# Memory's input and first weights take the places of x while the last projection pair runs

## The chip, the core and the metric

The kernel runs on one core of a Trainium2 chip. Five engines work side by side, each with its own queue of instructions in a fixed order: TensorE (PE; matmuls, with weight loads shown as PEld), VectorE (DVE), ScalarE (ACT), GpSimd (POOL) and SyncE (SP, which here issues all transfers). An instruction starts when those ahead of it in its queue have started and the tiles that it needs are ready; until then its queue stands. The metric is the device time of one execution in microseconds (us), lower is better.

## What is computed

One layer of a streaming encoder for 1024 prompt tokens and 64 sample tokens, width 1024, in fp32 accuracy. In outline:

```
h  = rms_norm(x);  p = h @ w_in                    # q, k, v of 8 A heads and 8 B heads, forget logits
x += concat(o_A, o_B) @ w_o                        # A: chunk band attention, B: forgetting attention
kv = rms_norm(mem) @ w_mkv                         # memory: 256 tokens, 4 heads of 256
mk, mv = rms_norm(kv[:, :1024] by head), kv[:, 1024:]
x += softmax(rms_norm(rms_norm(x) @ w_mq) @ mk.T / 16) @ mv @ w_mo
x += (silu(conv3(gate)) * value) @ w_down          # gate, value = rms_norm(x) @ w_up
```

The sample tokens do the same with keys and values from caches.

## The kernel before

**Exactness.** Each fp32 factor is split in a rounded part (hi, dtype F32R) and the rest (lo); a product is three matmuls, hi*hi, hi*lo and lo*hi. A split is one instruction on ACT (hi) and one on DVE or POOL (lo).

**The pairs.** The projection runs over eight pairs of heads p (0 to 3 of kind A, 4 to 7 of kind B) and, in each, over eight blocks t of 128 tokens. `products(p, t)` makes 24 matmuls of 384 columns (tile pj, line 299) from x's parts (xhi, xlo) and the pair's weights (whi, wlo). `proj` normalises q and k and turns them (tq, line 326). Woven between the matmuls of block t are the `substeps()` of the attention of blocks already projected, as an object `Attn(p, g, h)` for each group g of two blocks and head h: scores (tile S, line 499), their maximum (DVE, line 502), exponential (ACT, line 504), division (ACT or POOL), turning (PT, line 539; split by ACT, line 540, and DVE, line 541) and the product with v (tile O, one bank; line 554), which ACT (otmp, line 563) and DVE (mix, line 564) take out of the bank. `proj_sample` projects the sample tokens at a pair's end (line 347; sm, line 351).

**The drain.** After the last pair, attention has four substeps left. `step(n, subs)` weaves n pieces of the memory projection with one of them; `LEFT` holds the four n.

**Memory.** The projection of the 256 memory tokens has 16 units (n, t): eight blocks n of 256 columns of w_mkv, two blocks t of 128 tokens. A unit is four pieces of six matmuls of 256 columns (`mem_piece`, line 679), 384 in all. Its input is loaded in two halves (line 655), scaled and split into tiles mhi and mlo (`gained`, ACT line 265, DVE line 266). A block of weights is loaded in two halves (mwraw, line 661) and split in four pieces, mwhi on ACT (line 668) and mwlo on DVE and POOL in turn (line 669). `mem_end` normalises a unit into kv and stores it (out_mk, line 702); `mem_turn` turns it (PT, line 720) and stores it (kmd, line 723).

**Samples.** Eight samples follow, one for each pair. Each loads q, k, v of the sample (sqd, svn), its bias (s, from negs or rows), keys (kraw) and values (vraw) of the caches, splits them, and runs scores, exponential, turns, O and a last turn of the result su (line 857). They run as steps x; `PER[x]` says how many memory pieces are woven into step x. When no piece is left, the output product (line 948, tile a) starts.

**Order and memory.** A scheduler at build time fixes every queue's order from the program's order and the tiles that come free; a tile of a pool takes the place of one with the same tag that has been released. x's parts lie in two tiles [128, 8, 1024], which are released, with the pair weights, when all eight pairs are done (`left.close()`); memory's tiles are placed in that space afterwards.

Of the kernel before, what the change touches and what calls it, by code (L numbers as in the profile page):

```python
# [15 lines left out]
P = 128  # L16
# [10 lines left out]
LEFT = (0, 0, 0, 15)  # L27
PER = (4, 8, 9, 12, 6, 5, 6, 0, 0)
# [13 lines left out]
def hybrid_step(ctx: ExitStack, tc: tile.TileContext, i: dict, o: dict):  # L42
# [3 lines left out]
    def f32(ap):  # L46
        return ap.bitcast(F32)
# [125 lines left out]
    def split_col(c, k, raw):  # L173
        dst = [xs[:, k, a] for a in range(2)] if c == 4 else [a[:, k, c * 256:(c + 1) * 256] for a in x2]
        split_x(*dst, raw[:, k % 4], k, c == 0)
# [412 lines left out]
    def scale_gain():  # L588
# [5 lines left out]
             6: lambda: ([], norms(7, 8) + columns(4, 0) + columns(4, 1))}  # L594
    forgetting = []
    for p, np_ in zip(PAIRS, PAIRS[1:] + (None,)):
# [45 lines left out]
    left.close()  # L642


    left = ExitStack()
# [3 lines left out]
    mem = [mp.tile([P, KT, 256], F32R, name=f"m{n}") for n in ("hi", "lo")]  # L649
    gmk = mp.tile([P, 256], F32, name="gmk")  # L650
    nc.sync.dma_start(gmk, i["g_mk"].broadcast_to([P, 256]))

    def load_mem(z):
        raw = wk.tile([P, N], F32, name="s", bufs=4)[:, :1024].rearrange("p (k t) -> p k t", k=4)
        nc.sync.dma_start(raw, i["memT"][4 * z:4 * z + 4].rearrange("k p t -> p k t"))
        for k in range(4):
            gained((mem[0][:, 4 * z + k], mem[1][:, 4 * z + k], raw[:, k], gcol[:, 3, 4 * z + k:4 * z + k + 1], ALL))

    def load_wm(n, z):
        raw = mp.tile([P, 4, 256], F32, name="mwraw", bufs=2)  # L660
        nc.sync.dma_start(raw.rearrange("p k c -> p (k c)"), i["w_mkv"][n, z])
        wraw[n, z] = raw

    def split_wm(n, y):
        raw = wraw[n, y // 2][:, 2 * (y % 2):2 * (y % 2) + 2]
        hi = mp.tile([P, 2, 256], F32R, name="mwhi", bufs=6)
        lo = mp.tile([P, 2, 256], F32R, name="mwlo", bufs=6)
        act.copy(hi, raw)
        (dve if y % 2 else pool).tensor_tensor(lo, raw, f32(hi), op=ALU.subtract)
        wm.setdefault(n, []).append((hi, lo))  # L670

    wraw, wm, mpj = {}, {}, {}

    def mem_piece(n, t, c):
        if c == 0:
            mpj[n, t] = bank("pj")
        for m in range(6 * c, 6 * c + 6):
            k, (a, b) = m // 3, SPLIT[m % 3]
            mm = pe.matmul(mpj[n, t][:, :256], mem[a][:, k, t * P:(t + 1) * P], wm[n][k // 2][b][:, k % 2], start=m == 0, stop=m == 3 * KT - 1)
            if n + t + m == 0:  # L680
                tc.keep_in_program_order(mm)
# [203 lines left out]

    load_wm(0, 0)
    load_mem(0)
    load_wm(0, 1)
    load_mem(1)
    split_wm(0, 0)  # L890
    split_wm(0, 1)
# [1028 lines left out]
```

## Time and profile before

| | |
|---|---|
| time, median of 3 runs | 1780.92 us (1779.07 to 1783.11) |
| span of the profiled execution, first to last instruction | 1782.6 us |
| PE busy in the span | 1717.3 us, 12432 matmuls |
| DVE, ACT, POOL busy | 1217.0, 943.4, 646.1 us |
| moved by DMA | 199.88 MB, 112 GB/s in the mean |

The profile is of one execution. The time around its span is not shown apart: the span lies inside the range of the three runs, 1.7 us over their median, and the prediction's sum is made against it. In a row of a timeline stand: start, duration, engine, line, operation, out<-in, count, and in brackets the idle time ahead of it and what ended it. In a table of stretches each engine has its busy time and the number of its instructions, then the clock that PE was granted (1.00 is full), the DMA engines' busy share and GB/s. In a row of a tile's instructions the durations are ns, least/median/most.

### The profile page before, as it was taken

What the parts mean: (1) busy time and instruction counts of PE and PEld (TensorE: products, weight loads), DVE (VectorE), ACT (ScalarE), POOL (GpSimd) and SP (SyncE); (2) the same over time, 40 slices, a digit from 0 to 9 for tenths busy, and PEclk for the clock granted to TensorE, in tenths of its full rate; (3) what the DMA queues carried; (4) which work ended last, traced back from release to release, by engine and by line L of the source; (5) the groups of instructions that cost most, each with busy time, mean ns of one, the idle gap of its engine ahead of it and who ended that gap; (6) DMA issues with size and microseconds to landing.
All of it is one profiled execution on the core that took longest, in us unless ns stands there. A gap on an engine that the chain in (4) does not pass through costs nothing.

```text
span 1782.6 us, 34013 instructions
## 1 busy us (share of the span) xinstructions
PE 1717.3 (96%) x12432; PEld 1668.7 (94%) x12432; DVE 1217.0 (68%) x2659; ACT 943.4 (53%) x2074; POOL 646.1 (36%) x931
## 2 busy tenths in 40 slices
PE   7898999999998898999999999999999999999999
PEld 6888999999997787999999999999999999999999
DVE  5768667677677687533444379877777777649986
ACT  6756667677677577434555456433333333434432
POOL 3656667878777443443443611100000000000000
PEclk8999999999999899999999999999999999999999
DMA  7322122122112577641111563222222222693332
GB/s 246 99 63 62 59 77 79 49 74 77 50 55 81 175 259 248 194 140 46 54 54 54 153 217 103 76 80 73 83 82 89 82 73 73 226 339 130 118 105 88
DMA packets 136696, 199.88 MB, mean 112 GB/s; under 512 B 21240, under 2 KB 77688, under 8 KB 136528
## 3 DMA queue, kind: packets, MB, share of 16 engines
q1 hardware_dynamic: 136528, 197.70, 35.1%
q8 instruction: 98, 1.61, 0.4%
q14 instruction: 70, 0.57, 0.1%
HBM read 155.35 MB, written 45.44 MB: 113 GB/s over the span
## 4 chain that ended last, share of the span: by engine, by line
PE 49%; DVE 2%; issue 1%; POOL 1%; ACT 1%; DMA 0%; SPq 0%; DVEq 0%; POOLq 0%; ACTq 0%
PE W L1475 25%; PE W L1799 13%; PE pj L948 7%; PE S L1218 1%; PE tq L1254 1%; PE O L1254 1%; PE W L948 1%; POOL lo L930 1%; PE PT L1241 0%; DMA f<-x2d 0%; PE O L1218 0%; POOL s L1233 0%; PE PT L1199 0%; DVE lo L930 0%; ACT hi L929 0%
## 5 line engine op out<-in xcount | busy, mean ns | idle before, releaser
L299 PE MATMUL pj<-whi,xhi 128*128 128x384 f32 (+1 forms) x512 | 195.9, 383 | 2.2 <-ACT xhi L130 1.9
L299 PE MATMUL pj<-wlo,xhi 128*128 128x384 f32 (+1 forms) x512 | 176.9, 346 | 4.5 <-POOL wlo L123 4.5
L299 PE MATMUL pj<-whi,xlo 128*128 128x384 f32 (+1 forms) x512 | 176.3, 345 | 0.6 <-DVE xlo L131 0.6
L1581 POOL COPY s<-gp 128x2 f32<-128x2 f32 x22 | 15.8, 719 | 335.9 <-DVE gp L1580 335.9
L1475 PE MATMUL W<-h,hi 128*128 128x272 f32 x704 | 134.4, 288 | 1.4 <-ACT qlo L1611 1.4
L504 ACT ACTIVATE s<-s,mx 128x640 f32<-128x640 f32 (+7 forms) x128 | 94.4, 737 | 77.8 <-DVE mx L502 77.0
L1799 PE MATMUL W<-f,hi 128*128 128x272 f32 x672 | 127.1, 287 | 0.0
L541 DVE TENSOR_TENSOR ptl<-PT,pth 128x512 fp32r<-128x512 f32 (+2 forms) x192 | 99.4, 522 | 38.8 <-ACT pth L540 36.5
L1475 PEld LDWEIGHTS W<-h,hi 128*128 128x128 f32 x704 | 110.8, 188 | 1.7 <-ACT qlo L1611 1.6
L540 ACT CAST pth<-PT 128x512 fp32r<-128x512 f32 (+2 forms) x192 | 84.8, 449 | 43.8 <-PE PT L539 41.9
L299 PEld LDWEIGHTS pj<-wlo,xhi 128*128 128x128 f32 x512 | 99.6, 194 | 6.2 <-POOL wlo L123 6.1
L1799 PEld LDWEIGHTS W<-f,hi 128*128 128x128 f32 x672 | 105.3, 188 | 0.0
L299 PEld LDWEIGHTS pj<-whi,xhi 128*128 128x128 f32 x512 | 99.4, 194 | 4.4 <-ACT xhi L130 2.4
L1475 PE MATMUL W<-h,lo 128*128 128x272 f32 x352 | 101.8, 289 | 0.0
L299 PEld LDWEIGHTS pj<-whi,xlo 128*128 128x128 f32 x512 | 98.1, 192 | 1.8 <-DVE xlo L131 1.6
L539 PE MATMUL PT<-ident,s 128*128 128x128 f32 x528 | 90.5, 278 | 7.7 <-DVE ptl L541 7.3
L1799 PE MATMUL W<-f,lo 128*128 128x272 f32 x336 | 96.7, 288 | 0.0
L1339 ACT CAST hi<-raw 128x512 fp32r<-128x512 f32 x68 | 42.2, 621 | 98.5 <-PE W L1475 58.7
L948 PE MATMUL pj<-a,hi 128*128 128x384 f32 (+1 forms) x352 | 89.1, 336 | 2.5 <-ACT hi L929 1.6
L499 PE MATMUL S<-kh,q 128*128 128x256 f32 (+1 forms) x304 | 77.5, 280 | 13.1 <-DVE mx L502 13.1
L507 POOL TENSOR_SCALAR s<-s,ssum 128x640 f32<-128x640 f32 (+6 forms) x96 | 70.7, 738 | 47.5 <-DVE ssum L505 36.7
L554 PE MATMUL O<-pth,v 128*128 128x256 f32 (+1 forms) x304 | 78.0, 281 | 8.4 <-ACT mhi L265 7.7
(552 smaller groups left out, 6049.5 us busy)
## 6 DMA issues: line engine op xcount, KB each, us to landing
raw<-in_w_down_dram SPq DMA_DIRECT2D x45, 256.0 KB, 2.9
wraw<-in_w_dram SPq DMA_DIRECT2D x56, 192.0 KB, 2.5
raw<-in_w_up_dram SPq DMA_DIRECT2D x41, 256.0 KB, 2.7
h<-ad SPq DMA_DIRECT2D x32, 272.0 KB, 5.2
mwraw<-in_w_mkv_dram SPq DMA_DIRECT2D x16, 512.0 KB, 6.2
raw<-in_w_mo_dram SPq DMA_DIRECT2D x32, 256.0 KB, 3.2
kvraw<-in_w_down_dram SPq DMA_DIRECT2D x32, 256.0 KB, 3.1
ad<-t SPq DMA_DIRECT2D x22, 272.0 KB, 2.1
```

What stands on the lines that cost most here:

```text
L299: pe.matmul(pj[:, :nw], x2[a][:, k, t * P:(t + 1) * P], wt[k][b][:, :nw], start=n == 0, stop=n == 3 * KT - 1)
L499: pe.matmul(sp[:, a:a + (k1 - k0) * P], q, kk[:, h, src], start=m == 0, stop=m == 1)
L504: act.activation(s[:, :n], s[:, :n], ACT.Exp, bias=mx, scale=-1.0, accum_out=sm)
L507: pool.tensor_scalar(s[:, :n], s[:, :n], sm, 1.0, op0=ALU.mult, op1=ALU.mult)
L539: pe.transpose(pt[:, b - ch[0]], self.s[j][:, (b - w0) * P:(b - w0 + 1) * P], ident)
L540: act.copy(hi[:, f:f + n, j], pt[:, f:f + n])
L541: dve.tensor_tensor(lo[:, f:f + n, j], pt[:, f:f + n], f32(hi[:, f:f + n, j]), op=ALU.subtract)
L554: pe.matmul(op[:, cols], groups[p, b // 2].v[:, b % 2, h].rearrange("p a d -> p (a d)"), pt[:, x, cols], start=b == self.full[0] and m == ...
L948: pe.matmul(out()[:, :cn], w[a][:, k % 4], x[b][k][:, c0:c0 + cn], start=k == 0 and (a, b) == SPLIT[0], stop=k == KT - 1 and (a, b) == SPL ...
L1339: act.copy(hi, t)
L1475: pe.matmul(w[:, z, :Q], a(p, j), rights[j][b][:, z * Q:z * Q + Q], start=fresh and begin and j == 0 and x == 0, stop=final and end and j ...
L1799: pe.matmul(ws[m][:, z, :Q], la[p][:, m * P:(m + 1) * P], ra[b][:, z * Q:z * Q + Q], start=first and y == 0 and what in opening, stop=fina ...
```

## The change

x's parts become sixteen tiles of [128, 4, 256]: for each of hi and lo, four column blocks of 256 tokens times two halves of the depth, with the tags xhi and xlo, eight places each. When the last pair has used a tile for the last time, its place goes to one of memory's tiles of the same size: input (mraw), its parts, weights (mwraw), their parts. The pool of x stays open until the last memory piece; the pair weights' pool alone is closed. The input's loads and splits and the loads and splits of weight blocks 0 and 1 are called beside the last pair's blocks t = 2 to 7 (`beside`); the input no longer passes through a tile s of the attention. `LEFT` and `PER` spread the 65 memory steps anew: 23 in the drain instead of 15. A matmul that was held to the program's order no longer is.

```
-LEFT = (0, 0, 0, 15)
-PER = (4, 8, 9, 12, 6, 5, 6, 0, 0)
+LEFT = (4, 5, 6, 8)
+PER = (4, 6, 7, 8, 6, 5, 6, 0, 0)
...
-    wp = left.enter_context(tc.tile_pool(name="wp", bufs=1, side="left"))
-    x2 = [xp.tile([P, KT, T], F32R, name=f"x{n}") for n in ("hi", "lo")]
+    weights = ExitStack()
+    wp = weights.enter_context(tc.tile_pool(name="wp", bufs=1, side="left"))
+    def quarter_tile(part, name, dt=F32R):
+        return xp.tile([P, 4, 256], dt, name=name, tag=f"x{part}", bufs=8)
+    x2 = {}
+    def x_part(a, k, t0, n):
+        return x2[a, t0 // 256][k // 4][:, k % 4, t0 % 256:t0 % 256 + n]
...
-            pe.matmul(pj[:, :nw], x2[a][:, k, t * P:(t + 1) * P], wt[k][b][:, :nw], start=n == 0, stop=n == 3 * KT - 1)
+            pe.matmul(pj[:, :nw], x_part(a, k, t * P, P), wt[k][b][:, :nw], start=n == 0, stop=n == 3 * KT - 1)
...
+    def load_mem(z):
+        raw = raw_of["m", z] = quarter_tile(QUARTERS[z], "mraw", F32)
+        nc.sync.dma_start(raw, i["memT"][4 * z:4 * z + 4].rearrange("k p t -> p k t"))
+    def split_mem(k):
+        z, raw = k // 4, raw_of["m", k // 4]
+        if k % 4 == 0:
+            mem[z] = [quarter_tile(x, f"m{x}") for x in QUARTERS]
+        gained((mem[z][0][:, k % 4], mem[z][1][:, k % 4], raw[:, k % 4], gcol[:, 3, k:k + 1], ALL))
+    def load_wm(n, z):
+        raw = raw_of[n, z] = quarter_tile(QUARTERS[z], "mwraw", F32)
+        nc.sync.dma_start(raw.rearrange("p k c -> p (k c)"), i["w_mkv"][n, z])
...
+    beside = {2: [lambda z=z: load_mem(z) for z in range(2)], 4: [lambda z=z: load_wm(0, z) for z in range(2)],
+              6: [lambda z=z: load_wm(1, z) for z in range(2)], 7: [lambda y=y: split_wm(0, y) for y in range(4)]}
+    for z in range(2):
+        beside.setdefault(4 + z, []).extend(lambda k=k: split_mem(k) for k in range(4 * z, 4 * z + 4))
...
+            if np_ is None:
+                subs += beside.get(t, [])
...
-    left.close()
+    weights.close()
...
-            if n + t + m == 0:
-                tc.keep_in_program_order(mm)
...
-                if n == 0 and t == 0:
-                    if c < 2:
-                        split_wm(0, c + 2)
-                if n < 7:
-                    if t == 0 and c in (1, 2):
-                        load_wm(n + 1, c - 1)
-                    if t == 1:
-                        split_wm(n + 1, c)
+                if n < 7 and t == 1:
+                    split_wm(n + 1, c)
+                if n in range(1, 6) and t == 0 and c in (1, 2):
+                    load_wm(n + 2, c - 1)
...
-    load_wm(0, 0)
-    load_mem(0)
-    load_wm(0, 1)
-    load_mem(1)
-    split_wm(0, 0)
-    split_wm(0, 1)
+    for z in range(2):
+        load_wm(2, z)
```

The changed kernel's line numbers differ: the attention's are 11 higher (499 becomes 510, 554 becomes 565), those of kv, the samples and kmd 18 higher (702 becomes 720), and memory's functions now stand earlier (655, 661, 668, 669 and 679 become 611, 621, 629, 630 and 637).

The first place is ACT's queue at the end of the last pair, behind the sample's projection (sm). Before:

```order
L351 COPY sm<-pj 64x384
L265 ACTIVATE q<-tq,gd 128x2x128
L265 ACTIVATE mhi<-s,gcol 128x256
L233 ACTIVATE sq<-sm 64x256
L355 ACTIVATE vf<-sm,rstd_81 64x128
L265 ACTIVATE mhi<-s,gcol 128x256 x3
L668 CAST mwhi<-mwraw 128x512 x2
L563 COPY otmp<-O 64x256
L540 CAST pth<-PT 128x4x128 x2
```

In the changed kernel, at the same place:

```order
L362 COPY sm<-pj 64x384
L276 ACTIVATE q<-tq,gd 128x2x128
L244 ACTIVATE sq<-sm 64x256
L366 ACTIVATE vf<-sm,rstd_81 64x128
L574 COPY otmp<-O 64x256
L515 ACTIVATE s,ssum<-s,mx 128x896
L551 CAST pth<-PT 128x4x128
L520 ACTIVATE s<-s,ssum 128x896
L551 CAST pth<-PT 128x4x128
```

The splits of memory's input and of weight block 0 have moved ahead, between the blocks of the last pair; eight mhi and eight mwhi now stand before sm on ACT, eight mlo and four mwlo on DVE, four mwlo on POOL.

The second place is PE's queue in the drain, ahead of the first group of eight turns. Before:

```order
L554 MATMUL O<-pth,v 128x256
L554 MATMUL O<-ptl,v 128x256
L554 MATMUL O<-pth,v 128x128
L554 MATMUL O<-ptl,v 128x128
L539 MATMUL PT<-ident,s 128x128 x8
L554 MATMUL O<-pth,v 128x256
L499 MATMUL S<-kh,q 128x256
```

In the changed kernel, behind the same four O:

```order
L565 MATMUL O<-pth,v 128x256
L565 MATMUL O<-ptl,v 128x256
L565 MATMUL O<-pth,v 128x128
L565 MATMUL O<-ptl,v 128x128
L637 MATMUL pj<-mwhi,mhi 128x256
L637 MATMUL pj<-mwlo,mhi 128x256
L637 MATMUL pj<-mwhi,mlo 128x256
```

Groups of memory matmuls now stand between attention's groups. Counted over the whole order, 96 memory matmuls stand ahead of the last O (6 before), 128 from there to the first sample's turn of su (165 before), and 160 behind that (213 before).

The third place is SP's queue where the first sample's transfers stand. Before:

```order
L737 DMA sqd<-sqk 64x512
L702 DMA out_mk_dram<-kv 128x256
L661 DMA mwraw<-in_w_mkv_dram 128x1024
L723 DMA kmd<-kt 128x2x128
L739 DMA svn<-sv 64x128
L702 DMA out_mk_dram<-kv 128x256
L750 DMA kraw<-in_cbk_dram 128x1024
L723 DMA kmd<-kt 128x2x128
L750 DMA kraw<-in_cbk_dram 128x1024
L702 DMA out_mk_dram<-kv 128x256
L723 DMA kmd<-kt 128x2x128
L754 DMA vraw<-in_cbv_dram 128x512 x2
```

In the changed kernel:

```order
L720 DMA out_mk_dram<-kv 128x256
L741 DMA kmd<-kt 128x2x128
L755 DMA sqd<-sqk 64x512
L757 DMA svn<-sv 64x128
L768 DMA kraw<-in_cbk_dram 128x1024 x2
L772 DMA vraw<-in_cbv_dram 128x512 x2
```

Keys and values of the first sample stand together, behind the third pair of stores of kv and ahead of the fourth. Twelve of the sixteen weight loads (mwraw) now stand ahead of them, where six did.

More of the change, by code (lines that the diff above doesn't have):

```diff
@@ L173, in split_col @@
     def split_col(c, k, raw):
-        dst = [xs[:, k, a] for a in range(2)] if c == 4 else [a[:, k, c * 256:(c + 1) * 256] for a in x2]
+        if c < 4 and k % 4 == 0:
+            for a, part in enumerate(("hi", "lo")):
+                x2.setdefault((a, c), []).append(quarter_tile(part, f"x{part}"))
+        dst = [xs[:, k, a] for a in range(2)] if c == 4 else [x_part(a, k, c * 256, 256) for a in range(2)]
         split_x(*dst, raw[:, k % 4], k, c == 0)
@@ L641, in hybrid_step @@
             forgetting = forget()
-    left.close()
-    left = ExitStack()
+    weights.close()
     mp = left.enter_context(tc.tile_pool(name="mp", bufs=1, side="left"))
@@ L648, in hybrid_step @@
     vmd = dram.tile([2, P, T], F32, name="vmd")
-    mem = [mp.tile([P, KT, 256], F32R, name=f"m{n}") for n in ("hi", "lo")]
     gmk = mp.tile([P, 256], F32, name="gmk")
     nc.sync.dma_start(gmk, i["g_mk"].broadcast_to([P, 256]))
[L653 to L679, printed above, removed]
-            if n + t + m == 0:
-                tc.keep_in_program_order(mm)
     kvs, stores = {}, []
```

16 lines of the change are left out of this document (added).

## The prediction

> **What bounds the kernel now.** First the page of the profile: span, busy shares, and the 40 slices of 44.6 us each.
>
> ```profile
> span 1782.6 us, 34013 instructions
> PE 1717.3 (96%) x12432; PEld 1668.7 (94%) x12432; DVE 1217.0 (68%) x2659; ACT 943.4 (53%) x2074; POOL 646.1 (36%) x931
> PE   7898999999998898999999999999999999999999
> PEclk8999999999999899999999999999999999999999
> ```
>
> TensorE (PE) is the bound. It is below 9 tenths only at the start and in slices 13 to 16 (535 to 713 us), where its clock also falls. The change moves work only there, so I cut that place into stages, by what PE's timeline shows: the last pair, the attention that drains after it (566.3 is the end of the last projection, 601.1 the last O), the stretch to the end of the first sample's attention, and the other samples up to the first output product. A second table shows the clock.
>
> ```profile
> core 0: us, PE busy (x) PEld busy (x) DVE busy (x) ACT busy (x) POOL busy (x), PEclk, DMA share, GB/s
> 510.00:566.30 56.30, 55.66 (x384) 53.59 (x383) 37.43 (x109) 37.40 (x94) 39.77 (x80) 1.00 0.12 36
> 566.30:601.10 34.80, 22.53 (x142) 20.25 (x141) 25.55 (x47) 23.45 (x48) 19.39 (x26) 0.80 0.60 172
> 601.10:640.10 39.00, 34.46 (x243) 31.24 (x243) 29.27 (x76) 24.04 (x66) 17.32 (x20) 0.96 0.67 225
> 640.10:705.10 65.00, 60.25 (x427) 52.36 (x425) 46.18 (x116) 47.38 (x122) 25.43 (x21) 1.00 0.77 241
> ```
>
> ```profile
> 570.00:580.00 10.00, 1.92 (x9) 1.42 (x8) 7.99 (x13) 8.26 (x19) 7.23 (x10) 0.77 0.70 223
> 580.00:590.00 10.00, 7.78 (x43) 6.62 (x42) 8.62 (x16) 6.52 (x14) 6.81 (x8) 0.72 0.20 64
> 590.00:600.00 10.00, 8.03 (x51) 7.41 (x52) 5.98 (x13) 5.64 (x10) 3.95 (x5) 0.83 0.82 216
> ```
>
> In the last pair PE is full (55.66 of 56.30) and the other three engines have 16 to 19 us free each, the DMA nearly all. In the drain PE idles 12.3 us of 34.8. The PE rows say where:
>
> ```profile
> 578.01 0.55 PE L554 MATMUL O<-pth,v 128*128 128x256 f32 x1 [7.72 <-ACT mhi L265]
> ...
> 579.52 0.42 PE L499 MATMUL S<-kh,q 128*128 128x256 f32 x1
> 579.74 0.41 PE L499 MATMUL S<-kl,q 128*128 128x256 f32 x1
> ...
> 590.14 0.55 PE L539 MATMUL PT<-ident,s 128*128 128x128 f32 x3 [1.35 <-DVE ptl L541]
> 591.94 0.66 PE L539 MATMUL PT<-ident,s 128*128 128x128 f32 x4 [1.14 <-DVE ptl L541]
> ...
> 599.61 0.28 PE L679 MATMUL pj<-mwlo,mhi 128*128 128x256 f32 x1
> 599.73 0.28 PE L679 MATMUL pj<-mwhi,mlo 128*128 128x256 f32 x1
> ```
>
> One gap of 7.72 us; then matmuls of 256 columns start every 0.22 us (579.52 to 579.74) instead of every 0.12 (599.61 to 599.73). The gap's cause stands in ACT's and DVE's rows:
>
> ```profile
> 569.71 0.51 ACT L265 ACTIVATE mhi<-s,gcol 128x256 fp32r<-128x256 f32 x1 [0.62 <-DMA s<-in_memT_dram]
> 573.05 1.14 ACT L668 CAST mwhi<-mwraw 128x512 fp32r<-128x512 f32 x2 [1.04 <-DMA mwraw<-in_w_mkv_dram]
> 574.22 0.37 ACT L563 COPY otmp<-O 64x256 f32<-64x256 f32 x1
> 574.22 3.19 DVE L669 TENSOR_TENSOR mwlo<-mwraw,mwhi 128x512 fp32r<-128x512 f32 x1 [1.70 <-ACT mwhi L668]
> 577.45 0.42 DVE L564 TENSOR_TENSOR mix<-O,otmp 64x256 f32<-64x256 f32 x1
> ```
>
> The one O bank is free only after otmp and mix. Both stand in their queues behind the preparation of memory's input (mhi) and weights (mwhi, mwlo), which waits for its loads; the DVE split then took 3.19 us. So PE waits for work that it needs only at 599.5.
>
> **The drain (566.3 to 601.1).** The change takes all of this preparation out of the two queues: the 7.7 us gap goes, and what is late next is the chain scores, maximum, exponential, turn that the pauses of 1.35 and 1.14 show. A mean clock of 0.80 over 34.8 us is 13.9 us at half speed, of which some 11 lie outside the gap; PE idles in part of them anyway, so I give them 3 us (0 to 5.6). That leaves 24.1 us. Into it come, by the order, 96 memory matmuls before the last O instead of 6: 90 at 0.12 are 10.8. Attention's own 136 at 0.12 are 16.3. PE work is 27.1, over 24.1, so the stretch becomes PE's, with 1.5 us of pauses left: 28.6, that is -6.2. If all the added matmuls fit into pauses it is 24.1 (-10.7); if none does, 34.9 (+0.1).
>
> That the clock is lost with the gap is also what the Trainium skill says ("TensorE: Matmul & The Clock Gate", Part 1): about 3.4 us with little work halve it, about 3.4 us of work restore it. By that rule a drain whose pauses stay short runs at 1.00, and the 3 us are safe. The trace agrees at the long gap; but 590 to 600 shows 0.83 after two pauses of little over 1 us, so by the row some of the 3 us may come back.
>
> **To the first sample's end (601.1 to 640.1).** The order has 128 memory matmuls here instead of 165: 37 at 0.12, -4.4, since PE is busy 34.46 of 39.00. The rest:
>
> ```profile
> PE PT L720 <- DVE kv L701: 4.3, 4, 1.6
> 607.19 0.34 SPq L702 DMA_DIRECT2D out_mk_dram<-kv  x1
> 609.00 1.24 SPq L723 DMA_DIRECT2D kmd<-kt  x1
> 611.52 0.43 SPq L750 DMA_DIRECT2D kraw<-in_cbk_dram  x1
> 617.57 0.37 SPq L723 DMA_DIRECT2D kmd<-kt  x1
> 617.99 0.97 SPq L754 DMA_DIRECT2D vraw<-in_cbv_dram  x2
> ```
>
> PE waits 4.3 us for kv, the normalised memory keys; three of six such turns now fall into the drain beside attention, I take 2 us off. SP issues in order: the first sample's keys and values leave at 611.5 and 618.0, behind stores that wait for kv. Now they stand ahead of the fourth such store, so they can leave about 4 us after the last O instead of 10.4 and 16.9. PE waits little for them today, having memory matmuls to do, so I take 1.7 us: -8.1 in all. Bounds: -4.4 (all waits stay) to -13 (kv waits and sample waits go).
>
> **The other samples (640.1 to 705.1).** 160 memory matmuls instead of 213: 53 at 0.12 are 6.4. PE is busy 60.25 of 65.00, so nearly all should show: -6.0. But each sample is a chain through ACT and DVE, and the matmuls cover it: if the chains set the pace, 0. The weight loads now run ahead (12 of 16 issued before the first sample's keys, 6 before), which relieves a DMA share of 0.77; no PE wait on it is in the rows, so I count only up to 2 us: -8.
>
> **The last pair (510 to 566.3).** It takes the moved work:
>
> ```profile
> L265 ACT ACTIVATE mhi<-s,gcol x8: 491/499/516, 569.7 to 577.8; 128x256 fp32r<-128x256 f32 x8
> L266 DVE SCALAR_TENSOR_TENSOR mlo<-s,gcol,mhi x8: 469/476/486, 570.2 to 580.6; 128x256 fp32r<-128x256 f32 x8
> L668 ACT CAST mwhi<-mwraw x32: 602/617/631, 573.1 to 686.4; 128x512 fp32r<-128x512 f32 x32
> L669 DVE TENSOR_TENSOR mwlo<-mwraw,mwhi x16: 677/789/3195, 574.2 to 687.1; 128x512 fp32r<-128x512 f32 x16
> L669 POOL TENSOR_TENSOR mwlo<-mwraw,mwhi x16: 1262/1292/1749, 575.6 to 686.1; 128x512 fp32r<-128x512 f32 x16
> ```
>
> By the order eight mhi and eight mwhi go to ACT (4.0 + 4.9 = 8.9 us), eight mlo and four mwlo to DVE (3.8 + 3.2 = 7.0), four mwlo to POOL (5.2). Each engine has at least 16 us idle there, which is the cover; the loads have the DMA at 0.12. But the three run in order, and a turn that comes late stops PE. SP carries eight loads past the pair's stores, some waiting for a split; vf and ko have two buffers each, so a late store would hold ACT and POOL. I take +2. No PE work leaves this pair, so a gain is excluded; the upper bound is ACT's 8.9 laid bare.
>
> Sixteen tiles for x instead of two: the same matmuls in the same order up to the last pair, every slice inside one tile; 0. memory's raw input no longer takes two of the four s buffers: counted with the pauses.
>
> **Sum.** -6.2 - 8.1 - 6.0 + 2.0 = -18.3 on the span of 1782.6: 1764.3. The runs have a median of 1780.9 (1779.1 to 1783.1), 1.7 under that span, so the median becomes 1762.6; I say 1762.5.
>
> **Rivals.** (1) The chains set the pace of the samples: the last -6.0 is 0 and the stretch before gives only -4.4. For it: PT and ptl pauses wherever memory matmuls are few. Against: 60.25 of 65.00 busy. -6.2 - 4.4 + 2 = -8.6: 1772. (2) The pauses vanish everywhere: -10.7 - 13 - 8 + 0 = -31.7: 1749. Against it: kv's turns still stand behind only 18 to 29 matmuls, 2 to 3.5 us, where PE waits up to 1.6 today. (3) DVE is held in the last pair:
>
> ```profile
> L669 DVE TENSOR_TENSOR mwlo<-mwraw,mwhi 128x512 fp32r<-128x512 f32 x3 | 6.3, 2096 | 1.7 <-ACT mwhi L668 1.7
> L669 DVE TENSOR_TENSOR mwlo<-mwraw,mwhi 128x512 fp32r<-128x512 f32 x13 | 11.1, 856 | 0.5 <-ACT mwhi L668 0.5
> ```
>
> The same DVE split averages 2.10 us in the drain and 0.86 after it (0.68 at best); the longest, 3.19, runs while POOL works. The last pair has POOL busy 39.77 of 56.30. If each of the twelve moved DVE instructions is held as the three were (1.4 over the best) and PE pays, the pair costs 17 us: net -3.3, 1777.6. If each is held as the worst was (2.5), 30 us: net +9.7, 1790.6, slower. It decides from 1.7 us each. Against it: after the drain the hold is 0.18 a piece beside a POOL at 0.4, and DVE has 19 us free. The Trainium skill has such a rule ("SBUF — State Buffer", Who interferes with whom): a DVE instruction with two inputs in SBUF and a POOL instruction exclude each other for the whole instruction; the 3.19 us row agrees, the mean of 0.86 says that it seldom bites. (4) The gap only moves: memory matmuls stand right behind the last turns of the pair in PE's queue, and if their parts are late PE stops there instead: no change, 1781. Against: the parts are issued two steps and more earlier.
>
> **How the numbers follow.** Forecast as summed 0.62; (1) 0.16; (2) 0.12; (3) 0.06, half of it slower; (4) 0.04. The range 1746 to 1776 reaches from (2), with a little below it, past (1); it leaves out (3), (4) and the upper bounds all at once (0.1 - 4.4 + 0 + 8.9 = +4.6). About 0.2%, 3.6 us, is what a measurement here tells from no change. Faster 0.90; same 0.05; slower 0.05.
>
> **What would show it.** Right: no PE gap over 2 us after the last pair, clock near 1.00 from 566 to 600; mhi and the first mwhi before 566; memory matmuls between S and PT; last O near 597, the first sample's su turned near 628, the first output product near 687; the sample's keys issued within 5 us of the last O. Wrong: the last projection later than 569, DVE mwlo of 2 us in the last pair, PE waits on su, kclo or kv that grow by as much as the matmuls leave.

## The result, and the profile after

The changed kernel takes 1784.2 us (median of 21 runs, 1780.6 to 1785.9); the kernel before, run beside it, takes 1780.06 (21 runs, 1777.7 to 1783.5). The ratio is 1.0019 [1.0013, 1.0026]: slower by 0.19%, a little under what the prediction took as measurable, where 1762.5 was forecast.

The page of the changed kernel: span, PE's busy share, its 40 slices, the granted clock.

```profile
span 1781.2 us, 34032 instructions
PE 1714.3 (96%) x12432; PEld 1666.1 (94%) x12432; DVE 1216.3 (68%) x2659; ACT 942.3 (53%) x2074; POOL 644.8 (36%) x931
PE   7898999999999888999999999999999999999998
PEclk8999999999999998999999999999999999999999
```

PE's row was below 9 in slices 13, 14 and 16; now it is in 14, 15 and 16 (44.5 us each) and in the last. The clock's dip has moved from slice 14 (579 to 624 us) to slice 16 (668 to 712), into the samples. The four stages of the changed kernel (last pair, drain, to the first su, other samples), by the columns of the prediction's tables:

```profile
496.10:570.40 74.30, 69.94 (x474) 65.53 (x473) 55.09 (x146) 55.82 (x135) 57.64 (x99) 1.00 0.36 109
570.40:602.80 32.40, 29.30 (x239) 27.84 (x238) 25.58 (x59) 22.91 (x56) 17.55 (x25) 1.00 0.41 115
602.80:635.90 33.10, 28.65 (x210) 25.65 (x209) 25.81 (x70) 20.73 (x55) 14.67 (x18) 0.99 0.81 258
635.90:704.50 68.60, 58.88 (x365) 50.22 (x363) 46.23 (x107) 44.75 (x113) 24.52 (x22) 0.90 0.64 201
```

Before, the same stages took 68.8, 34.9, 39.0 and 65.1 us. The drain's clock went from 0.80 to 1.00 and its 7.72 us gap is gone, as forecast. The last pair got 5.5 us longer, and the samples 3.5 us longer, with 53 memory matmuls fewer and a clock of 0.90 where there was 1.00.

The profile of before that the prediction used was of a long execution: its span and the 1.8 us around it make 1784.4, 4.3 over the median of 21 runs. The first experiment below (e3) has the order of before in every queue; its stages, also of one execution, show how far two such profiles differ:

```profile
496.90:565.60 68.70, 67.94 (x473) 65.48 (x472) 48.38 (x134) 48.44 (x119) 50.68 (x96) 1.00 0.15 46
565.60:598.30 32.70, 20.79 (x143) 17.86 (x142) 22.28 (x49) 23.48 (x48) 18.64 (x24) 0.84 0.64 184
598.30:635.70 37.40, 33.45 (x244) 29.92 (x243) 29.44 (x75) 24.02 (x65) 18.33 (x23) 1.00 0.71 236
635.70:700.90 65.20, 60.64 (x429) 52.50 (x426) 46.37 (x117) 47.48 (x122) 25.46 (x21) 1.00 0.74 240
```

The drain of before was 2.2 us longer and the next stretch 1.6, with the same order: chance between executions. Against e3 the change moves the stages by +5.6, -0.3, -4.3 and +3.4: +4.4 in all, which fits the 4.1 us between the medians.

### The profile page after: what moved, and what is told of

Its sections match the earlier page's. It is cut to its first block, busy times and chain, and to the rows that moved or that the text cites. A ratio compares the mean times of both kernels' runs of the same rounds, so it can differ in the third digit from the quotient of the medians.

```text
span 1781.2 us, 34032 instructions
## 1 busy us (share of the span) xinstructions
PE 1714.3 (96%) x12432; PEld 1666.1 (94%) x12432; DVE 1216.3 (68%) x2659; ACT 942.3 (53%) x2074; POOL 644.8 (36%) x931
## 4 chain that ended last, share of the span: by engine, by line
PE 51%; DVE 1%; POOL 1%; issue 1%; ACT 0%; DVEq 0%; POOLq 0%; ACTq 0%
PE W L1485 25%; PE W L1809 13%; PE pj L958 7%; PE W L958 2%; PE S L1228 1%; PE tq L1264 1%; PE O L1264 1%; POOL lo L940 1%; PE PT L1251 0%; PE O L1228 0%; PE PT L1209 0%; POOL s L1243 0%; DVE f L1350 0%; ACT hi L939 0%; DVE qhi L1337 0%
## 5 line engine op out<-in xcount | busy, mean ns | idle before, releaser
L550 PEld LDWEIGHTS PT<-ident,s 128*128 128x128 f32 x528 | 65.5, 140 | 14.9 <-DVE ptl L552 9.1
```

The costliest lines, as they stand in the source:

```text
L550: pe.transpose(pt[:, b - ch[0]], self.s[j][:, (b - w0) * P:(b - w0 + 1) * P], ident)
```

## The experiments

All runs in one table: us by stage, the clock and the memory matmuls (M) in the samples and M in the drain, each from the one profile of that kernel. Ratios are against the kernel before, run beside each.

| kernel | median us, runs | ratio, 95% interval | pair | drain | to su | samples | clock | M drain, samples |
|---|---|---|---|---|---|---|---|---|
| before | 1780.06, 21 | | 68.8 | 34.9 | 39.0 | 65.1 | 1.00 | 6, 213 |
| changed | 1784.20, 21 | 1.0019 [1.0013, 1.0026] | 74.3 | 32.4 | 33.1 | 68.6 | 0.90 | 96, 160 |
| e3 | 1780.19, 11 | 1.0000 [0.9991, 1.0008] | 68.7 | 32.7 | 37.4 | 65.2 | 1.00 | 6, 213 |
| e1 | 1771.91, 5 | 0.9950 [0.9937, 0.9962] | 75.5 | 26.1 | 34.7 | 62.2 | 1.00 | 45, 208 |
| e2 | 1786.08, 7 | 1.0029 [1.0017, 1.0040] | 68.8 | 41.2 | 32.8 | 68.5 | 0.95 | 96, 165 |
| e4 | 1782.82, 11 | 1.0014 [1.0006, 1.0023] | 68.9 | 41.1 | 34.4 | 64.6 | 0.95 | 96, 161 |
| e6 | 1778.54, 11 | 0.9989 [0.9980, 0.9997] | 71.9 | 32.8 | 34.9 | 66.8 | 0.93 | 54, 204 |
| e7 | 1778.80, 12 | 0.9997 [0.9988, 1.0005] | 68.9 | 33.6 | 31.9 | 71.4 | 0.97 | 62, 214 |
| e8 | 1782.89, 12 | 1.0014 [1.0004, 1.0025] | 76.8 | 31.9 | 34.0 | 67.0 | 0.95 | 54, 204 |
| e9 | 1775.91, 11 | 0.9979 [0.9971, 0.9988] | 78.1 | 26.1 | 34.8 | 62.4 | 1.00 | 45, 208 |
| e12 | 1787.63, 5 | 1.0043 [1.0031, 1.0055] | 73.8 | 33.6 | 37.0 | 68.8 | 0.95 | 96, 171 |
| e11 | 1775.85, 7 | 0.9975 [0.9963, 0.9987] | 73.6 | 29.5 | 33.9 | 65.8 | 0.97 | 48, 216 |
| e13 | 1773.15, 6 | 0.9962 [0.9949, 0.9975] | 72.4 | 28.4 | 33.7 | 64.6 | 1.00 | 48, 216 |
| e14 | 1771.02, 5 | 0.9950 [0.9938, 0.9963] | 73.1 | 26.0 | 35.0 | 62.2 | 1.00 | 45, 208 |
| e15 | 1772.60, 5 | 0.9956 [0.9943, 0.9968] | 75.6 | 25.8 | 30.9 | 66.3 | 0.97 | 45, 228 |
| e18 | 1778.27, 11 | 0.9990 [0.9981, 0.9999] | 74.4 | 36.7 | 32.8 | 60.2 | 0.94 | 132, 119 |
| e19 | 1773.84, 5 | 0.9965 [0.9953, 0.9978] | 75.6 | 31.6 | 33.8 | 60.8 | 0.95 | 96, 160 |
| e20 | 1777.15, 11 | 0.9987 [0.9978, 0.9995] | 74.4 | 32.5 | 33.9 | 62.5 | 0.97 | 96, 168 |
| e21 | 1766.58, 5 | 0.9926 [0.9912, 0.9939] | 73.1 | 26.1 | 32.0 | 62.4 | 1.00 | 47, 206 |
| e22 | 1763.70, 4 | 0.9903 [0.9887, 0.9920] | 72.8 | 25.7 | 32.1 | 61.1 | 1.00 | 47, 208 |

**The parts of the change, each alone.** e3: before with the sixteen tiles.

```
-    x2 = [xp.tile([P, KT, T], F32R, name=f"x{n}") for n in ("hi", "lo")]
+    def quarter_tile(part, name, dt=F32R):
+        return xp.tile([P, 4, 256], dt, name=name, tag=f"x{part}", bufs=8)
...
-            pe.matmul(pj[:, :nw], x2[a][:, k, t * P:(t + 1) * P], wt[k][b][:, :nw], start=n == 0, stop=n == 3 * KT - 1)
+            pe.matmul(pj[:, :nw], x_part(a, k, t * P, P), wt[k][b][:, :nw], start=n == 0, stop=n == 3 * KT - 1)
```

> The kernel before with x's parts in sixteen tiles alone; every queue has the same order as before. If the tiles cost nothing: 1780, ratio 0.999 to 1.001, and its profile is a second look at the kernel before (last pair 68 to 69.5, drain 34 to 36, 39 and 65 us for the two other stretches); what differs there by more is chance between executions. Rival (the sixteen tiles cost time by themselves, in the places or addresses of the operands): 1782 to 1784, with the eight pairs longer by 2 to 4 us in all.

1780.19: the tiles cost nothing. e2: before with the new spread alone; e1: the changed kernel with the old one.

```
 e2 (on before)                              e1 (on the changed kernel)
-LEFT = (0, 0, 0, 15)                       -LEFT = (4, 5, 6, 8)
-PER = (4, 8, 9, 12, 6, 5, 6, 0, 0)         -PER = (4, 6, 7, 8, 6, 5, 6, 0, 0)
+LEFT = (4, 5, 6, 8)                        +LEFT = (0, 0, 0, 15)
+PER = (4, 6, 7, 8, 6, 5, 6, 0, 0)          +PER = (4, 8, 9, 12, 6, 5, 6, 0, 0)
```

> The kernel before with the new LEFT and PER alone: x stays in two tiles, memory's input and weights are loaded and split behind the last pair as before, one block ahead, in pieces of half a quarter tile. Last pair 68 to 69 us, since nothing is added to it. The gap of 7.7 us ahead of the drain's scores remains, and 96 memory matmuls stand ahead of the last O: drain 36 to 44 us (34.9 before, 32.4 changed). Theory 2a (too few matmuls cover the samples): from the first su to the first output product 66 to 69 us with waits for kclo, as in the changed kernel (68.6). Theory 2b (fours of splits): 59 to 61 us, as I had forecast, because the splits stay spread one by one. Total by 2a 1781 to 1786, by 2b 1776 to 1780.

> The changed kernel with the old LEFT and PER: memory's input and weights still take x's places and are split beside the last pair, but 15 memory steps instead of 23 go into the drain and the samples get the old numbers. By the order 45 memory matmuls stand ahead of the last O (96 changed, 6 before), 131 from there to the first su, and the samples 5 to 1 keep 38, 62, 53, 26, 29 of them (16, 47, 46, 20, 31 in the changed kernel). Theory 1 (the splits in the last pair hold the q/k chain there): the last pair stays at 73 to 75 us (68.8 before, 74.3 changed). Theory 2a (the samples were lost because too few memory matmuls cover the chains): from the first su to the first output product less than 1 us of PE waits on kclo, total time 1778 to 1780, under before. Theory 2b (the samples were lost because the weights' splits come in fours ahead of kclo): the fours remain, DVE's mwlo and kclo still take 1.3 us and more beside POOL, total time 1782 to 1785. If the new spread was good in itself, 1786 or more.

The new spread is what made the change slower: without it the changed kernel takes 1771.9, 8.6 us under before; put alone into the kernel before it makes that slower by 0.29%. In e1 48 more memory matmuls stand in the samples, and that stage is 6.4 us shorter; 51 fewer stand in the drain, which is 6.3 us shorter, 0.12 each. e1 was faster than either of its theories had it. In e2 the samples are as long as theory 2a had them (68.5), but PE waits there for POOL's mwlo (3.8 us in three waits), not for kclo.

**What the last pair pays for.** e4: the changed kernel with the loads beside the last pair and all splits behind it (anchor[0] is the copy sm).

```
-        act.copy(hi, raw)
+        with tc.issue_after(anchor[0].ins) if n < 2 else ExitStack():
+            act.copy(hi, raw)
...
-    for z in range(2):
-        beside.setdefault(4 + z, []).extend(lambda k=k: split_mem(k) for k in range(4 * z, 4 * z + 4))
...
+    with tc.issue_after(anchor[0].ins):
+        for k in range(KT):
+            split_mem(k)
+    for y in range(4):
+        split_wm(0, y)
```

> The changed kernel with only the loads of memory's input and of weight blocks 0 and 1 beside the last pair; all their splits (8 mhi, 16 mwhi, 8 mlo, 16 mwlo) are held behind the copy of the last pair's sample projection (sm), as before. Theory 1 (the splits in the last pair hold the q/k chain on ACT, DVE and POOL): the last pair returns to 68 to 70 us; the rival (the loads and their places, or SP's order, do it): it stays at 73 to 75. In the drain the splits stand ahead of otmp again without the 1.7 us of waiting for loads, 24 instead of 10 on ACT: a gap of 6 to 10 us comes back, drain 38 to 44. The samples as in the changed kernel (67 to 70 us from first su to first output product). Total 1782 to 1787; by the rival 1787 to 1792.

68.9: the loads and their places are free, and the splits cost the pair the 5.4 us. Behind the pair they cost the drain 8.7. The samples took 64.6 us, where 67 to 70 were expected; that comes up again below. How they cost the pair is in PE's and POOL's rows. The changed kernel:

```profile
534.54 0.73 POOL L496 TENSOR_SCALAR s<-bias,ctok 128x512 f32<-128x512 f32 x1 [0.81 <-PE PT L550]
535.24 1.04 POOL L261 TENSOR_TENSOR r<-m,mhalf 128x4 f32<-128x4 f32 x1
536.25 0.37 POOL L497 TENSOR_SCALAR_AFFINE_SELECT s<-s 128x128 f32<-128x128 f32 x1
536.61 1.63 POOL L263 TENSOR_SCALAR qk<-qkraw,r 128x128 f32<-128x128 f32 x4
...
537.26 1.37 PE L337 MATMUL tq<-ident,qk 128*128 128x128 f32 x4 [1.77 <-POOL qk L263]
```

e4 at the same block:

```profile
533.37 1.02 POOL L261 TENSOR_TENSOR r<-m,mhalf 128x4 f32<-128x4 f32 x1 [2.30 <-DVE m L260]
534.48 1.41 POOL L263 TENSOR_SCALAR qk<-qkraw,r 128x128 f32<-128x128 f32 x4
...
534.91 1.37 PE L337 MATMUL tq<-ident,qk 128*128 128x128 f32 x4
```

The mhi and mlo stand between ACT's and DVE's steps of the q and k chain, so m comes 1.3 us later; in the built order a bias step and its select stand around POOL's r, and qk starts 2.1 us later. PE's turn tq then waits 1.77 us. Two such waits (2.2 us), two for mx (1.2) and one for ptl (0.8) are the 4.2 us of waits that PE's rows show, against 0.7 before. The rest is busy time, 1.9 us more at the same number of matmuls (68.02 to 69.94): 1.1 of it in the turns tq (5.1 to 6.2 us), where each turn of a group of four waits for its piece of qk. No engine was full: ACT 55.8, DVE 55.1, POOL 57.6 of 74.3.

e6 keeps the input's splits beside the pair and puts the weights' behind it, e7 puts all behind it (as e4); both with the old spread.

```
 e6: e4's edit without the part on split_mem, and both:
-LEFT = (4, 5, 6, 8)
-PER = (4, 6, 7, 8, 6, 5, 6, 0, 0)
+LEFT = (0, 0, 0, 15)
+PER = (4, 8, 9, 12, 6, 5, 6, 0, 0)
```

> The changed kernel with the old LEFT and PER (as e1_old_spread, 1771.9) and the weights' splits of blocks 0 and 1 held behind the copy sm: only the input's splits (mhi, mlo) stay beside the last pair, at blocks 4 and 5. Theory 1: the last pair loses at two places, some 2.5 us at 530 to 540 (input: POOL gives r and qk late, PE waits for them ahead of tq) and some 3 us at 550 to 570 (weights). So the last pair is 71 to 72 us (75.5 in e1, 68.8 before), without the waits at 567 and 569. The weights' splits now stand in the drain: 26.1 us becomes 28 to 33. Total 1770 to 1775. Rival: the input's splits alone hold the pair (74 to 76) or the weights' alone do (69).

> As e4_loads_only (only loads beside the last pair, all splits behind sm), with the old LEFT and PER. It parts the two halves of what the old spread gains: if the samples gain through the memory steps that cover them (theory 2a), the stretch from first su to the first output product is 60 to 64 us at a clock of 0.98 and more, against 64.6 at 0.95 in e4, and the drain shrinks from 41.1 to 33 to 37 us, by the memory matmuls that leave it (62 by the order ahead of the last O instead of 96, 34 at 0.12 are 4 us). Last pair 68.9. Total 1771 to 1776. If the spread matters only together with splits in the last pair, 1780 to 1784.

Pair and drain came as expected (71.9 and 32.8; 68.9 and 33.6): about 3 us are the input's, 3.6 the weights'. Both totals came some 3 us above the forecast, since I had not foreseen the samples (66.8 and 71.4 us, 62.2 in e1). With the spread of e1 their splits, loads and stores fall elsewhere, and e7 waits 4.4 us for su; more of it is not explained.

e8 and e9 call the input's splits earlier and spread out, on e6 and on e1.

```
-        beside.setdefault(4 + z, []).extend(lambda k=k: split_mem(k) for k in range(4 * z, 4 * z + 4))
+    for k in range(KT):
+        beside.setdefault(3 + k // 2, []).append(lambda k=k: split_mem(k))
```

> As e6_input_only, with the input's eight splits called two beside each of blocks 3, 4, 5 and 6 instead of four beside blocks 4 and 5. POOL's order has one bias step instead of two ahead of r at the place where PE waited 1.77 us for qk. Theory 1: that wait goes, last pair 69 to 70 us, total 1 to 3 us under e6. Rival (any split in the pair costs its own time on ACT or DVE): the same pair as in e6, same total.

> As e1_old_spread, with the input's splits called two beside each of blocks 3 to 6; the weights' splits stay beside block 7. Last pair 72 to 74 us (75.5 in e1): the wait for qk at 537 goes (1.8 to 2.3 us), those at 553 to 571 stay; drain 26 to 27. Total 1769 to 1771 against 1771.9. If the wait only moves: 1771 to 1773.

Both missed: the pair got longer (76.8, 78.1). e9's rows:

```profile
519.49 0.51 ACT L276 ACTIVATE mhi<-mraw,gcol 128x256 fp32r<-128x256 f32 x1 [3.32 <-DMA mraw<-in_memT_dram]
...
524.51 0.47 PE L550 MATMUL PT<-ident,s 128*128 128x128 f32 x1 [3.07 <-DVE ptl L552]
```

The wait for qk fell to 0.86 us as expected, but the first mhi now stood at the head of ACT's queue and waited 3.32 us for its load, and PE paid 3.07: the gap of before in small. In e8 PE waits 3.6 us for ptl there.

e11 and e13 hold the splits to the program's order, as x's and the pair weights' already are, two to a block, on e1; e13 calls them ahead of the block's attention. e14 holds only the input's and weight block 0's (named mvhi and mvlo there). In all three the input is called as in e8, weight block 0 two pieces beside block 6 and two beside 7.

```
+ORDERED |= {"Activation mhi", "DVE mlo", "Activation mwhi", "DVE mwlo", "Pool mwlo"}
 e13, e14 also:
-                subs += beside.get(t, [])
+                subs = beside.get(t, []) + subs
```

> e1_old_spread (1771.9) with the splits held to the program's order as in e12 and called two to a block: the input's beside blocks 3 to 6, weight block 0's beside 6 and 7, each behind the attention of its block. Now no split can slip ahead of its block and wait there for its load, which cost e9 3.1 us at 524. Last pair 70 to 73 us (75.5 in e1), the rest as in e1: total 1767 to 1771. Rival (each split costs what it takes on ACT and DVE, wherever it stands): 75 us again, 1771 to 1774.

> As e11_in_order_spread, with each block's splits called ahead of its attention instead of behind it, so that ACT and DVE have them right behind the q and k chain of the block before, with most of a block (8.6 us) until the next chain. Last pair 69 to 71 us, rest as in e1: total 1765 to 1769. Rival as in e11: 75 us, 1771 to 1774.

> Joins the last pair of e13 (72.4 us) with the rest of e1 (26.1, 34.7 and 62.2 us): the splits of memory's input and of weight block 0 are held to the program's order, two to a block, ahead of the block's attention; the splits of weight blocks 1 to 7 are free as in e1; old LEFT and PER. If the stages add up: 72.5 to 74 for the last pair (four more mwhi come back into it), 26 to 27 for the drain, 97 behind it, total 1769 to 1771, under e1 (1771.9). Rival (the four mwhi cost the pair what e13 saved): 75.5 and 1772 again.

The pair took 73.6, 72.4 and 73.1; in e11 and e13 it fell less than expected, and they lost more in drain and samples than they won, so that their totals missed too. e14 added up and ties with e1 within the runs' spread.

How much of the pair is place? The order of PE, DVE, ACT and POOL up to the end of the pair is the same in the changed kernel, e1, e15, e18, e19 and e20, and each shows the wait of 1.77 or 1.78 us for qk. Yet the pair takes 74.3, 74.4 and 74.4 us in the changed kernel, e18 and e20, and 75.5, 75.6 and 75.6 in e1, e15 and e19: in these three the clock fell behind that wait. The 10 us around it, in the changed kernel and in e1:

```profile
530.00:540.00 10.00, 7.66 (x44) 6.38 (x44) 6.96 (x25) 6.67 (x21) 6.50 (x14) 1.00 0.31 86
530.00:540.00 10.00, 7.73 (x40) 6.46 (x39) 6.89 (x25) 6.53 (x21) 6.47 (x13) 0.88 0.28 86
```

So 1.2 us of what e1's pair pays is chance. e14's pair, at a clock of 1.00, is 1.2 us under the changed kernel's, which is what place was worth; 4.3 over before stay.

**The price of a memory matmul.** e12 tests whether the fours of weight splits cost the samples (the changed kernel with e11's ORDERED and the new spread), e15 and e18 change the spread of e1.

```
 e15: LEFT = (0, 0, 0, 8)   PER = (4, 9, 11, 14, 8, 6, 5, 0, 0)
 e18: LEFT = (6, 7, 8, 10)  PER = (4, 5, 6, 5, 5, 4, 5, 0, 0)
```

> The changed kernel (new LEFT and PER) with all splits of memory's input and weights (mhi, mlo, mwhi, mwlo) held to the program's order on their engines, as the splits of x and of the pairs' weights already are. Only four mwhi, two mwlo on DVE and two on POOL stay in the last pair; in the samples the weights' splits stand where the program writes them instead of as soon as their places are free. Theory 2b (the fours of splits ahead of kclo cost the samples): from first su to first output product 62 to 65 us (68.6 changed), less than 2 us of waits for kclo, total 1776 to 1780. Theory 2a (too few memory steps cover the samples): 66 to 70 us, total 1781 to 1785.

> e1_old_spread with 8 memory steps in the drain instead of 15 (LEFT 0, 0, 0, 8; PER 4, 9, 11, 14, 8, 6, 5). By the order the drain keeps its 45 memory matmuls, the stretch to the first su has 111 instead of 131, and the samples 228 instead of 208 (160 in the changed kernel). Theory 2a: a memory matmul in the samples is free as long as PE has waits there; e1's PE idles only 4.8 us of 62.2, so this is near the end of the free ones. Stretch to the first su 32 to 34 (34.7), samples 62 to 65 (62.2), total 1769 to 1773. If they were free without end 1769.5, if they cost 0.12 us each everywhere, the same total as e1.

> e1_old_spread with 31 memory steps in the drain instead of 15 (LEFT 6, 7, 8, 10; PER 4, 5, 6, 5, 5, 4, 5): by the order 132 memory matmuls ahead of the last O (45 in e1, 96 in the changed kernel), 133 to the first su, 119 in the samples (208 and 160). Theory 2a (in the drain a memory matmul costs its 0.12 us, in the samples nothing, since their chain through ACT and DVE sets the pace): drain 36 to 38 us, samples 63 to 68, total 1782 to 1788. By the price that my prediction used (0.12 us at either place): samples 51 to 55, total 1770 to 1774.

In the drain 45, 96 and 132 memory matmuls make 26.1, 32.4 and 36.7 us: 0.12 each, the full price. In the samples 119 (e18) and 208 (e1) make 60.2 and 62.2: 0.02 each. Their rows, e18 first:

```profile
640.90:701.10 60.20, 52.62 (x330) 42.92 (x328) 43.07 (x108) 43.36 (x110) 22.48 (x24) 0.94 0.70 217
632.40:694.60 62.20, 57.39 (x412) 50.54 (x411) 45.93 (x113) 45.31 (x115) 27.13 (x24) 1.00 0.75 228
```

e18's clock is 0.94; if all of that 0.06 (3.6 us) were lost time, the price would be 0.06, an estimate and still half of 0.12. e18's total fell between the two theories: no kernel here has samples under 60.2 us, whatever their number of matmuls, which is lower than I had it. The price is that of these two kernels. Of the others most lie above the line through them, up to 9 us (e7, with 214), so the number alone does not set this stage; and why 228 (e15) make 66.3, one run does not tell. The changed kernel, with 160, lies 7.5 us above the line, and e12, in order, was as long (its stretch to the first su is 3.9 us longer too, and its total above both theories): holding the splits to the program's order did not help.

**What made the samples longer.** PE's waits for kclo in the samples (us in total, times, longest), before, in e1 and in the changed kernel, and two places in DVE's and POOL's queues of the changed kernel (vc is the lo half of the values):

```profile
PE S L807 <- DVE kclo L785: 0.3, 1, 0.3
PE S L825 <- DVE kclo L803: 0.2, 1, 0.2
PE S L825 <- DVE kclo L803: 4.2, 4, 1.9
```

```profile
650.76 3.13 DVE L630 TENSOR_TENSOR mwlo<-mwraw,mwhi 128x512 fp32r<-128x512 f32 x2
653.81 3.46 DVE L803 TENSOR_TENSOR kclo<-kraw,kchi 128x512 fp32r<-128x512 f32 x2
...
650.36 2.98 POOL L630 TENSOR_TENSOR mwlo<-mwraw,mwhi 128x512 fp32r<-128x512 f32 x2 [2.74 <-ACT mwhi L629]
653.41 3.32 POOL L811 TENSOR_TENSOR vc<-vraw,vc 128x512 fp32r<-128x512 f32 x2
```

The wait at 673 and what follows it, and the clock of 670 to 680:

```profile
673.31 0.79 PE L825 MATMUL S<-kclo,sq 128*128 128x512 f32 x1 [1.93 <-DVE kclo L803]
673.90 0.41 PE L637 MATMUL pj<-mwhi,mhi 128*128 128x256 f32 x1
674.11 0.41 PE L637 MATMUL pj<-mwlo,mhi 128*128 128x256 f32 x1
```

```profile
670.00:680.00 10.00, 8.07 (x37) 7.10 (x38) 6.00 (x11) 3.16 (x8) 4.84 (x4) 0.66 0.33 101
```

A pair of mwlo or kclo on DVE takes 3.1 to 3.5 us here, about as long as POOL's pair beside it; alone it takes 1.3. Of the 20 such pieces that DVE makes in this stage, the eight that began while POOL was making a lo half took 1.37 to 1.78 us, the other twelve 0.68 or 0.69. PE waits for kclo, and behind the 1.93 us wait its matmuls of 256 columns start every 0.21 us instead of every 0.12.

The hold is not all of it. e4 has nearly the same number of matmuls (161), the same kclo (0.998 us in the mean) and nearly the same waits for it, but none over 1.14 us:

```profile
PE S L826 <- DVE kclo L804: 3.6, 4, 1.1
640.30:704.90 64.60, 56.05 (x366) 47.38 (x364) 45.66 (x105) 44.09 (x111) 24.37 (x22) 0.95 0.67 210
```

Its samples are 4.0 us shorter, and its clock stays 1.00 from 660 to 700, where the changed kernel's is 0.50 from 674 to 678. So about half of the 7.5 us goes with that dip of the clock, as far as one profile of each can tell. e19 gives every lo half from block 2 on to DVE, e20 to POOL.

```
-        (dve if y % 2 else pool).tensor_tensor(lo, raw, f32(hi), op=ALU.subtract)
+        (dve if y % 2 or n > 1 else pool).tensor_tensor(lo, raw, f32(hi), op=ALU.subtract)   # e19
+        (dve if y % 2 and n < 2 else pool).tensor_tensor(lo, raw, f32(hi), op=ALU.subtract)   # e20
```

> The changed kernel with the lo half of every weight split from block 2 on made by DVE; before, DVE and POOL took them in turn. Theory 2c (in the samples POOL's mwlo and DVE's mwlo and kclo hold each other: kclo takes 1.00 us in the mean there against 0.69 in e1, and PE waits 4.2 us for it): without POOL's mwlo kclo returns to 0.7 to 0.8 us and DVE's mwlo to 0.7 to 0.9, the waits for kclo fall under 2 us, the stretch from first su to first output product to 62 to 66 us (68.6), total 1778 to 1782. Rival 2d (what counts is how much DVE has to do ahead of kclo): six more mwlo on DVE, waits for kclo of 4 us and more, 68 to 71 us, total 1784 to 1788.

> The changed kernel with the lo half of every weight split from block 2 on made by POOL. DVE has six mwlo less in the samples, POOL six more of 1.5 us. Theory 2c: kclo still meets POOL's mwlo, so it takes 1.0 us and more in the mean and PE waits 3 us or more for it: 67 to 71 us, total 1784 to 1788. Rival 2d: kclo comes earlier, waits under 2 us, 62 to 66 us, total 1778 to 1782.

The DVE groups in the samples, of the changed kernel:

```profile
L803 DVE TENSOR_TENSOR kclo<-kraw,kchi 128x512 fp32r<-128x512 f32 x14 | 13.7, 995 | 0.9 <-ACT kchi L802 0.8
L630 DVE TENSOR_TENSOR mwlo<-mwraw,mwhi 128x512 fp32r<-128x512 f32 x6 | 7.6, 1288 | 0.5 <-ACT mwhi L629 0.3
```

and of e19:

```profile
L803 DVE TENSOR_TENSOR kclo<-kraw,kchi 128x512 fp32r<-128x512 f32 x14 | 9.4, 687 | 1.2 <-ACT kchi L802 1.2
L630 DVE TENSOR_TENSOR mwlo<-mwraw,mwhi 128x512 fp32r<-128x512 f32 x12 | 8.6, 757 | 0.0
```

The samples of e19:

```profile
637.60:698.40 60.80, 55.54 (x366) 47.67 (x364) 42.29 (x111) 44.45 (x113) 15.39 (x17) 0.95 0.71 225
```

Twice as many mwlo on DVE, and DVE is busy 18.0 us with both instead of 21.3; PE's rows show no wait for kclo any more; the samples take 60.8, on the line between e18 and e1. The median is 10.4 us lower by this one edit, more than either theory had (the two profiled executions differ by 7.2, 6.6 of them in the four stages). e20 also helped (62.5), as only the rival had it, and its total too was below both forecasts: kclo still took 0.90 us there, held by POOL, but DVE had no mwlo ahead of it, and PE's waits for it fell to 1.5 us. I read this as both counting: the hold makes DVE's pieces longer, and what stands ahead of kclo decides whether PE sees it. The Trainium skill ("SBUF — State Buffer", Who interferes with whom) says that a DVE instruction with two inputs in SBUF and a POOL instruction that reads SBUF contend; the 0.995 and 0.687 agree.

**A version that beats both.** e21 is e14 with e19's edit; e22 makes every lo half of memory's weights on DVE.

```
 e21: +        (dve if y % 2 or n > 1 else pool).tensor_tensor(lo, raw, f32(hi), op=ALU.subtract)
 e22: +        dve.tensor_tensor(lo, raw, f32(hi), op=ALU.subtract)
```

> e14_pair_of_e13 (1771.0) with the lo half of weight splits from block 2 on made by DVE, as in e19. In e14 the samples have few waits for kclo (0.2 us) and 62.2 us at a clock of 1.00, so theory 2c leaves little to gain: 1770 to 1772. Rival 2d: DVE late, 1773 to 1776.

> e21_best_lo_on_dve (1766.6) with the lo halves of weight blocks 0 and 1 made by DVE as well, so that POOL makes none in the last pair either. In e21 a DVE instruction of the q and k chain that takes 0.28 us took 1.30 beside POOL's mvlo (545.75 beside 545.60), and mwlo on DVE took 1.78 beside POOL's at 563.99. Theory 2c: these holds go, last pair 70 to 72 us (73.1), total 1763 to 1766. Rival (DVE is the late engine there, with four more pieces of 0.69 us): 74 to 76 us, total 1767 to 1770.

e21 takes 1766.6, where I had expected next to nothing: its samples stayed (62.4), but the stretch to the first su, which neither theory had looked at, fell from 35.0 to 32.0. e22 takes 1763.7 us, 0.97% under before. Its stages:

```profile
494.80:567.60 72.80, 68.97 (x475) 65.53 (x474) 56.86 (x150) 55.57 (x136) 54.34 (x96) 1.00 0.34 108
567.60:593.30 25.70, 23.45 (x186) 21.73 (x185) 20.70 (x47) 19.68 (x42) 15.61 (x24) 1.00 0.43 119
593.30:625.40 32.10, 30.21 (x214) 26.69 (x213) 26.17 (x75) 22.53 (x61) 9.50 (x12) 1.00 0.84 265
625.40:686.50 61.10, 57.50 (x413) 50.66 (x412) 47.53 (x121) 45.44 (x115) 14.58 (x17) 1.00 0.76 235
```

The clock is 1.00 in all four. In the last pair the hold was the small part: 73.1 to 72.8, where I had expected 1 to 3 us. That the total came as forecast (1763 to 1766) is luck: the largest part lies in the samples (62.4 to 61.1). That pair's remaining 4 us are not settled; its rows show waits for mx (2.3 us) and qk (1.0).

## Why the prediction was wrong, term by term

**The last pair, +2: measured +5.5.** The step that failed was the cover: I set the engines' idle 16 to 19 us against 5 to 9 us of moved work. That idle time lies between the steps of a chain, and a piece of 0.5 us that stands in the wrong place delays the chain's next step, whatever the total: the rows show it for qk. The last projection starts at 570.4, past the 569 that I had named as a sign of being wrong. e4 shows that the splits are the cost; which chain holds the 4.3 us that e14 still pays is open. Rival (4), a gap that only moves, did not come; rival (3), DVE held by POOL, is a small part here (e22) and counts in the samples, where I had not put it.

**The drain, -6.2: measured -2.5, and -0.3 against e3.** The first half of the mechanism held: no gap, clock 1.00. What failed is the filling. I let the 90 added matmuls fill pauses, down to 1.5 us; measured, the 32.4 us hold 5.3 more than the 27.1 of counted work. By e1, e18 and the changed kernel each memory matmul added its full 0.12, on some 20.7 us without any (26.1 less 45 times 0.12, an estimate): the pauses stayed. And the 34.9 that I started from was 2.2 us longer than e3's.

**To the first su, -8.1: measured -5.9, -4.3 against e3.** Against e3 that is about the 4.4 of the 37 matmuls, the bound at which all waits stay. They did nearly: PE waits 3.2 us for kv, after 4.3 (3.7 in e3), where I took 2 off. The keys of the first sample, forecast 4 us behind the last O, are issued 10.0 us behind it (10.5 before): two of the three pairs of kv's stores ahead of them go out only 3.7 to 8.4 us behind the last O.

**The other samples, -6.0: measured +3.5.** This is the largest miss, over 9 us of the 22 between forecast and result. I took the busy share, 60.25 of 65.00, to mean that each matmul costs its 0.12 us there. But PE is busy there because the matmuls are woven into the waits of a chain; taken out, they leave the waits. From e1 to e18 89 of them took 2.0 us along, not 10.7, so at that price (0.02, at most 0.06) the 53 were worth 1 to 3 us; this is rival (1), to which I gave 0.16. On top of it came time that no term had, though waits for kclo were among my signs of being wrong: DVE and POOL, making lo halves side by side, made kclo late, and behind the longest wait the clock fell (0.90 in the mean). e19 takes the hold away and lands on the line. Why the new spread sets those pieces side by side, when e1 has kclo at 0.688, is not shown.

The old spread with the new places (e1) is the faster kernel. The range was too narrow because my worst ends were priced inside one mechanism each; a loss in the samples was not among them.

## What to carry to other kernels

Ahead of moving filler work from one stage to another, ask in each stage what it would be without the filler, and measure it with two spreads: where a chain through other engines sets the pace, filler is nearly free and its removal saves little. The busy share does not tell: in e1 PE is busy 57.39 of 62.20 us in the samples, where a matmul cost 0.02, and 22.76 of 26.10 in the drain, where it cost its full 0.12. Work moved beside a chain is priced by what stands behind it in each queue, not by the idle sum. And a split shared in turn by DVE and POOL can be slower than the same split on DVE alone.

## What the runs showed of the hardware

- A DVE subtraction of 128x512 with both inputs in SBUF takes 0.68 us alone and, in the changed kernel's samples, 1.4 to 1.8 where it begins while POOL makes one (3.19 once in the drain of before, beside several of POOL's); giving DVE twice as many and POOL none cut DVE's own busy time in the samples from 21.3 to 18.0 us.
- The granted clock fell in the samples with waits that were short one by one: 0.81 us ended at 669.9 and 1.93 us at 673.3, then 0.50 from 674 to 678. With one order of instructions and one wait of 1.77 to 1.78 us it fell in three of six executions (e1, e15 and e19, not the changed kernel, e18 and e20), which made 1.2 us. By the Trainium skill ("TensorE: Matmul & The Clock Gate", Part 1) it takes an idle window of about 3.4 us; these rows had less in one piece.
- Two profiles of the same order of instructions (before and e3) differed by 3.8 us in the drain and the stretch behind it, while e1, e9 and e14 agree within 0.3 us in the three stages behind the pair.
